# Head sums and low-rank products of an RWKV preparation as float32r parts, on one core of a Trainium2 chip

## The chip, the cores and the metric

The kernel runs on one core of a Trainium2 chip. The core has TensorE (PE, with its weight loads PEld), VectorE (DVE), ScalarE (ACT), GpSimdE (POOL) and the DMA queues, one of them issued by SyncE (SP). The metric is the device time of one execution in microseconds.

## The reference

One decoder layer: 512 tokens of width 1024, float32. A normed input is projected once; its columns feed a sparse attention mixer, an RWKV-7 mixer and two gates. The mixers are merged, projected, added to the input, and a gated MLP with a short convolution follows. What matters here is the preparation of the RWKV mixer (8 heads of 64):

```python
r, k, v, xw, xa, xg = jnp.split(xl, RWKV_SPLITS, axis=-1)
w = -jax.nn.softplus(-(w0 + jnp.tanh(xw) @ w2)) - 0.5
decay = jnp.exp(-jnp.exp(w.astype(jnp.float32)))
a = jax.nn.sigmoid(a0 + xa @ a2)
...
kk = k * k_k.reshape(H, N).astype(jnp.float32)
kk = kk / jnp.maximum(jnp.sqrt(jnp.sum(kk * kk, axis=-1, keepdims=True)), 1e-12)
k = k * (1.0 + (a - 1.0) * k_a.reshape(H, N).astype(jnp.float32))
...
y = y + jnp.sum(r * k * r_k, axis=-1, keepdims=True) * v
```

`tanh(xw) @ w2` and `xa @ a2` are the low-rank products (inner width 64 each). The two `jnp.sum` over the 64 channels of a head are the head sums: one for the norm of `kk`, one for the bonus.

## The kernel before

Activations lie feature-major: 128 features on the partitions, 512 tokens along the free side, so one tile holds two heads, and four pairs p = 0 to 3 hold the eight. Dense products (`dense_fm`) keep about float32 accuracy with float32r operands: weights and activations are split into a high part, rounded to float32r (`whi`, `hh`), and the rest (`wlo`, `hl`), and three products are added up, hi x hi, hi x lo and lo x hi. For one `dense_fm` that is 16 products that take `whi` and 8 that take `wlo`, 24 of 128x128 by 128x512. ScalarE makes `whi` and VectorE (at times GpSimdE) makes `wlo`, two buffers of each; SyncE's queue loads `raw` into three buffers.

The preparation runs over p. `front(p)` makes `k` (`kx`) by a dense product, then the two low-rank products into `ps_a` and `ps_b`: `wa` holds `w2` on partitions 0 to 63 and `a2` on 64 to 127, `xw` holds `tanh(xw)` and `xa` likewise, so each product uses 64 rows of the array. Then come the decay, its running sum along each chunk of 64 tokens (`cum`, by a scan), and its exponentials `ep` and `pi`. `norms(p)` squares `k` on ScalarE and multiplies the squares by `ones`, a 128x128 matrix with ones where two partitions belong to the same head: the head sum, spread over the head's partitions. `receptance(p)` and `values_of(p)` are dense products that give `rx` and `vx`. `values_tok(p)` transposes `vx`. `vectors(p)` makes `AR`, `bh` and the bonus sum (`tv` times `ones`, into `BO`). `gram(p)` transposes `bh` in sixteen 64-row operations, eight for each head of the pair, into one `ps_a` and one `ps_b` bank, and then multiplies `bh` by `AR` in sixteen 64-row products, first into another pair of `ps_a` and `ps_b`, then into two `ps_mm` banks; VectorE masks them into `AB`.

The program calls `front(0)`, `norms(0)`, `receptance(0)`, `values_of(0)`, and then for each p: `front(p+1)`, `norms(p+1)`, `values_tok(p)`, `vectors(p)`, `receptance(p+1)`, `gram(p)`, `values_of(p+1)`; one more dense product (`kcp`) comes at p = 2. In this part a scheduler orders each engine's instructions when the kernel is built; an engine runs its queue in that order. PSUM has two banks for `pa()` (`ps_a`), two for `pb()` (`ps_b`) and four for `mmb()` (`ps_mm`); a bank is free again when its last reader is done. After the preparation VectorE inverts the chunk matrices, while TensorE goes on with dense products, and from there on TensorE's order is mostly written out by hand.

In the profile nearly all matrix products have line L120 (the helper `mm`), ScalarE's activations L123 (`act`), VectorE's operations L126, L130, L132 and L135 (`tt`, `ts`, `stt`); L294 is the weight split on VectorE or GpSimdE, L540 the transposes of `vx`, L571 those of `bh`. `kc` holds the constants, `ones` among them.

Of the kernel before, what the change touches and what calls it, by code (L numbers as in the profile page):

```python
# [10 lines left out]
F32 = mybir.dt.float32  # L11
F32R = mybir.dt.float32r
I32 = mybir.dt.int32
AF = mybir.ActivationFunctionType
ALU = mybir.AluOpType
# [4 lines left out]
S = 512  # L20
# [27 lines left out]
NROWS = _n  # L48
NR0 = ROWS["ffn_norm_g"][0]
# [31 lines left out]
def hybrid_block(ctx: ExitStack, tc: tile.TileContext, A: dict, out: bass.AP):  # L81
    nc = tc.nc
# [16 lines left out]
    def pool(name, side="left"):  # L99
        cm = tc.tile_pool(name=name, bufs=1, side=side)  # L100
        return cm, cm.__enter__()

    def close(cm):
        cm.__exit__(None, None, None)


    def bank(tag, bufs, shape=(128, 512)):
        return ps.tile(list(shape), F32, name="ps_" + tag, tag=tag, bufs=bufs)

    def mmb():  # L110
        return bank("mm", 4)

    def pa():
        return bank("a", 2)

    def pb():
        return bank("b", 2)

    def mm(o, l, r, start, stop):
        te.matmul(o, lhsT=l, rhs=r, start=start, stop=stop)  # L120

    def act(o, i, f=AF.Copy, **kw):
        sc.activation(o, i, f, **kw)  # L123

    def tt(o, a, b, op):
        v.tensor_tensor(o, a, b, op=op)  # L126

    def ts(o, a, s1, s2, op0=ALU.mult, op1=ALU.add):
        if s2 is None:
            v.tensor_scalar(o, a, s1, None, op0=op0)  # L130
        else:
            v.tensor_scalar(o, a, s1, s2, op0=op0, op1=op1)  # L132

    def stt(o, a, s, b, op0=ALU.mult, op1=ALU.add):
        v.scalar_tensor_tensor(o, a, s, b, op0=op0, op1=op1)  # L135
# [3 lines left out]
    ident, mask, ones, cmask = kc[:, 0:128], kc[:, 128:256], kc[:, 256:384], kc[:, 384:416]  # L139
# [16 lines left out]
    for name in ("rwkv_mu", "rwkv_w0", "rwkv_a0", "rwkv_k_k", "rwkv_k_a", "rwkv_r_k", "rwkv_ln_g", "rwkv_ln_b"):  # L156
        r0, n = ROWS[name]
        src = A[name]
        if name == "rwkv_r_k":
            src = src.rearrange("l h d -> l (h d)")  # L160
# [7 lines left out]
    def col(name, i=0):  # L168
        r0, n = ROWS[name]
        return prm[:, r0 + i:r0 + i + 1]  # L170
# [35 lines left out]
    def norm_tiles(pool_):  # L206
        return (cp.tile([128, NT, 2], F32, name="ss", tag="ss"),
                [pool_.tile([128, D], F32, name="h", tag="h", bufs=NT) for _ in range(NT)])
# [120 lines left out]
    with tc.manual_schedule(engines={getattr(mybir.EngineType, e) for e in ("PE", "Activation", "DVE", "Pool")}):  # L329
# [18 lines left out]
        hi = wp.tile([128, KT, 128], F32R, name="whi", tag="whi", bufs=2)  # L348
        lo = wp.tile([128, KT, 128], F32R, name="wlo", tag="wlo", bufs=2)
# [43 lines left out]
    def run(g):  # L393
        while True:
            try:
                next(g)
            except StopIteration as e:
                return e.value

    def dense_fm_g(xh, xl, kt=KT):  # L400
        hi, lo = wnext(kt, 128)
        p = mmb()
        for k in range(kt):
            mm(p, hi[:, k], xh[:, k], k == 0, False)
            mm(p, hi[:, k], xl[:, k], False, False)
            if 4 * k == 3 * kt - 4:
                yield
        for k in range(kt):
            mm(p, lo[:, k], xh[:, k], False, k == kt - 1)
        return p  # L410

    def dense_fm(xh, xl, kt=KT):
        return run(dense_fm_g(xh, xl, kt))


    gp_cm, gp = pool("tb", "right")
# [3 lines left out]
    tp_cm, tp = pool("rtmp")  # L420
# [6 lines left out]
    BO = gp.tile([128, 4, S], F32, name="BO", tag="BO")  # L427
    PC = rp.tile([128, NH2, NCH], F32, name="PC")
    sg = gp.tile([128, S], F32, name="sg", tag="sg")
    g2 = gp.tile([128, 512], F32, name="g2", tag="g2")  # L430
    scanm = tp.tile([128, NCH, C], F32, name="scanm")
    v.memset(scanm, 1.0)
    v.memset(scanm[:, :, 0:1], 0.0)
    wa = tp.tile([128, 512], F32, name="wa")
    nc.gpsimd.dma_start(wa[0:64], A["rwkv_w2"][0])
    nc.gpsimd.dma_start(wa[64:128], A["rwkv_a2"][0])
    nc.gpsimd.dma_start(g2, A["rwkv_g2"][0])

    def shift_mix(p, m, dst):
        mu = col("rwkv_mu", m)  # L440
        act(dst, p, AF.Copy, scale=omm[:, m:m + 1])
        stt(dst[:, 1:], p[:, :-1], mu, dst[:, 1:])

    def t2(name, bufs=1):
        return tp.tile([128, S], F32, name=name, tag=name, bufs=bufs)

    xw = t2("xw")
    shift_mix(p0, 12, xw)
    act(xw[0:64], xw[0:64], AF.Tanh)
    shift_mix(dense_fm(hh, hl), 13, sg)  # L450

    act(sg, sg, AF.Tanh, scale=0.5)
    ts(sg, sg, 0.25, 0.25)


    prb = tp.tile([NROWS - NR0, 128], F32, name="prb")
    for name, (r0, n) in ROWS.items():
        if r0 >= NR0:
            r0 -= NR0
            src = A[name]  # L460
            if name.startswith("cmp_pe"):
                src = src.rearrange("l a d -> l (a d)")
# [2 lines left out]
                nc.gpsimd.dma_start(prb[r0:r0 + 1, 64:128], src)  # L465
            else:
                nc.gpsimd.dma_start(prb[r0:r0 + n], src[0].rearrange("(r p) -> r p", p=128))
    cr = tp.tile([88, 2, 128], F32, name="cr")
    nc.gpsimd.dma_start(cr[0:44, 0], A["conv_w"][0, 0].rearrange("(r p) -> r p", p=128))
    nc.gpsimd.dma_start(cr[44:88, 0], A["conv_w"][0, 1].rearrange("(r p) -> r p", p=128))  # L470
    nc.gpsimd.dma_start(cr[0:44, 1], A["conv_w"][0, 2].rearrange("(r p) -> r p", p=128))
# [1 line left out]
    def chunks(ap):  # L473
        return ap.rearrange("p (c t) -> p c t", t=C)
# [12 lines left out]
    L = {}  # L487


    def front(p):  # L490
        cs = slice(128 * p, 128 * p + 128)
        kx = t2("kx", 2)
        pk = dense_fm(hh, hl)
        zw, za = pa(), pb()
        mm(zw, wa[0:64, cs], xw[0:64], True, True)
        mm(za, wa[64:128, cs], xw[64:128], True, True)
        shift_mix(pk, 4 + p, kx)
        cl = t2("cl")
        act(cl, zw, AF.Tanh, scale=0.5, bias=w0h[:, p:p + 1])
        aa = t2("aa", 2)  # L500
        act(aa, za, AF.Tanh, scale=0.5, bias=a0h[:, p:p + 1])
        ts(cl, cl, -0.5 * DECAY, -0.5 * DECAY)
        cum = t2("cum")
        v.tensor_tensor_scan(out=cum, data0=scanm.rearrange("p c t -> p (c t)"), data1=cl, initial=0.0,
                             op0=ALU.mult, op1=ALU.add)
        ep = tp.tile([128, NCH, C + 1], F32, name="ep", tag="ep", bufs=2)
        v.memset(ep[:, :, 0:1], 1.0)
        act(ep[:, :, 1:], chunks(cum), AF.Exp)
        pi = t2("pi", 2)
        act(pi, cum, AF.Exp, scale=-1.0)  # L510
        v.tensor_copy(PC[:, p, :, None], ep[:, :, C:C + 1])
        L[p] = dict(kx=kx, aa=aa, ep=ep, pi=pi)

    def norms(p):
        kx = L[p]["kx"]
        kk = t2("kk", 2)
        act(kk, kx, AF.Square, scale=col("rwkv_k_k", p))
        ss = pa()
        mm(ss, ones, kk, True, True)
        rn = t2("rn", 2)  # L520
        ts(rn, ss, 1e-24, None, op0=ALU.max)
        act(rn, rn, AF.Ln)
        act(rn, rn, AF.Exp, scale=-0.5)
        L[p].update(kk=kk, rn=rn)

    def receptance(p):
        rx = t2("rx", 2)
        shift_mix(dense_fm(hh, hl), p, rx)
        L[p]["rx"] = rx

    def values_of(p):
        vx = t2("vx")
        shift_mix(dense_fm(hh, hl), 8 + p, vx)
        L[p]["vx"] = vx
# [9 lines left out]
                    pt[64 * cc:64 * cc + 64].rearrange("p (c r d) -> p c r d", r=2, d=DH)[:, :, r, :])  # L544

    def vectors(p):
        kx, aa, ep, pi, kk, rn, rx, vx = (L[p][k] for k in ("kx", "aa", "ep", "pi", "kk", "rn", "rx", "vx"))
        stt(AR[:, p, :, 1, :], chunks(rx), 1.0, ep[:, :, 1:], ALU.mult, ALU.mult)
        stt(kk, kx, col("rwkv_k_k", p), rn, ALU.mult, ALU.mult)
        stt(AR[:, p, :, 0, :], chunks(kk), -1.0, ep[:, :, 0:C], ALU.mult, ALU.mult)  # L550
        stt(kk, aa, 1.0, kk, ALU.add, ALU.mult)
        bh = tp.tile([128, NCH, 3, C], F32, name="bh", tag="bh")
        stt(bh[:, :, 0, :], chunks(kk), 0.5, chunks(pi), ALU.mult, ALU.mult)
        v.tensor_copy(bh[64:128, :, 2, :], bh[64:128, :, 0, :])
        ts(aa, aa, kah[:, p:p + 1], oma[:, p:p + 1])
        stt(kx, kx, 1.0, aa, ALU.mult, ALU.mult)
        stt(bh[:, :, 1, :], chunks(kx), 1.0, chunks(pi), ALU.mult, ALU.mult)
        tv = t2("tv")
        stt(tv, rx, col("rwkv_r_k", p), kx, ALU.mult, ALU.mult)
        L[p]["bh"] = bh  # L560
        bs = pa()
        mm(bs, ones, tv, True, True)
        tt(BO[:, p], bs, vx, ALU.mult)

    def gram(p):
# [19 lines left out]


    front(0)
    norms(0)
    receptance(0)
    values_of(0)  # L590
    late_params()
    for p in range(NH2):
        if p + 1 < NH2:
            front(p + 1)
            norms(p + 1)
        values_tok(p)
        vectors(p)
        if p + 1 < NH2:
            receptance(p + 1)
        gram(p)  # L600
        if p + 1 < NH2:
            values_of(p + 1)
        if p + 2 == NH2:
            kcp = dense_fm(hh, hl)
    dbg("AR", AR)
    dbg("BO", BO)
    close(tp_cm)

    m2_cm, m2 = pool("mix2")
    sg_cm, sgp = pool("sig")  # L610
    spare = sgp.tile([128, 2, 1024], F32R, name="spare", tag="sg0")
    sg1 = sgp.tile([128, 4, S], F32, name="sg1", tag="sg1")
    tp_cm, tp = pool("rinv")
# [163 lines left out]
    tp_cm, tp = pool("rseq")  # L777
# [455 lines left out]
    for m in range(KT):  # L1233
        cs = slice(128 * m, 128 * m + 128)
# [13 lines left out]
    ss, hs = norm_tiles(ntp)  # L1248
# [36 lines left out]
    with tc.manual_schedule(engines=KTS):  # L1285
        for t in range(NT):
            qs = slice(128 * t, 128 * t + 128)
            p = mmb()
# [13 lines left out]
        for pair in range(2):  # L1302
            cs = slice(256 * pair, 256 * pair + 256)
# [37 lines left out]
    for hf in range(2):  # L1341
        bo = dense_tok(512, aT[:, 0], aT[:, 1], NF)
        for t in range(NT):
            n = 256 if hf and t == NT - 1 else 512
            for c0 in range(0, 512, n):
                cs = slice(512 * hf + c0, 512 * hf + c0 + n)
# [30 lines left out]
```

## Time and profile before

| | |
|---|---|
| median of 3 runs | 848.09 us (847.67 to 848.52) |
| profiled execution | 847.76 us |
| its span | 846.0 us |
| granted TensorE clock | 1.00 |
| stretch with the changed code | about 18 to 125 us of the span |
| TensorE busy in 18 to 125 us | 106.31 us of 107.00 |
| VectorE, ScalarE busy there | 75.80 us, 66.89 us |

The span runs from the first to the last instruction. A row of the timeline has the start, the duration, the engine, the line, the operation, output <- inputs, the array's rows*columns for a product, the output's shape and type, and the count; in brackets stand the engine's idle time before it and what ended it. TensorE's records overlap: a product's duration includes its passage through the array, and the distance from one start to the next is what it costs in a dense sequence. Float32r operands of products are shown as f32. A float32 product has two records.

### The profile page before, as it was taken

To read this page: it belongs to the slowest core of one execution; us is meant where nothing else is said; L and a number is where in the kernel's file an instruction comes from. 1 tells how busy PE (TensorE), PEld (TensorE's weight loads), DVE (VectorE), ACT (ScalarE), POOL (GpSimd) and SP (SyncE) were. 2 spreads that over 40 slices of the span, in tenths; PEclk is the share of its full clock that TensorE was granted. 3 is DMA by queue.
4 is the path that set the end of the run, shared out by engine and by line. 5 is a ranking of instruction groups with operands and counts; after the bars stand their busy time and mean duration, and the time that the engine had idled before them with its cause. 6 is when DMAs were issued, how large, how long until landed. Compare 5 with 4: busy or idle time off the path is not lost.

```text
span 846.0 us, 12844 instructions
## 1 busy us (share of the span) xinstructions
PE 831.9 (98%) x5097; PEld 676.2 (80%) x5097; DVE 514.7 (61%) x998; ACT 405.7 (48%) x784; POOL 52.5 (6%) x69
## 2 busy tenths in 40 slices
PE   7999999999999999999999999999999999999998
PEld 6777778897777886777788888888888888888886
DVE  5477779963555678888675566666666666322222
ACT  6766645443545677767344454444444444221210
POOL 6200020140000110111000000000000000000000
PEclk9999999999999999999999999999999999999999
DMA  7432222335551320010167023333333332333421
GB/s 231 112 86 62 75 75 76 92 108 151 132 119 50 83 69 13 15 36 26 52 215 221 0 77 98 100 100 100 100 100 95 90 91 98 100 100 112 136 75 50
DMA packets 109104, 78.73 MB, mean 93 GB/s; under 512 B 3869, under 2 KB 97748, under 8 KB 109044
## 3 DMA queue, kind: packets, MB, share of 16 engines
q1 hardware_dynamic: 106512, 73.51, 29.8%
q0 software_dynamic: 1472, 1.86, 1.0%
q10 hardware_dynamic: 1060, 2.55, 1.0%
q8 instruction: 40, 0.66, 0.3%
q14 instruction: 20, 0.16, 0.1%
HBM read 74.56 MB, written 2.29 MB: 91 GB/s over the span
## 4 chain that ended last, share of the span: by engine, by line
PE 52%; DVE 0%; ACT 0%; DVEq 0%; issue 0%
PE ps_mm L120 52%; DVE hl L135 0%; PE ps_a L120 0%; PE ps_b L1181 0%; PE ps_a L200 0%; PE ps_mm L1181 0%; ACT hh L123 0%; PE ps_b L200 0%; DVE x L126 0%; DVEq L1373 0%; PE ps_a L1133 0%
## 5 line engine op out<-in xcount | busy, mean ns | idle before, releaser
L294 DVE TENSOR_TENSOR wlo<-raw,whi 128x1024 fp32r<-128x1024 f32 (+1 forms) x111 | 131.6, 1185 | 189.4 <-PE ps_mm L120 166.8
L120 PE MATMUL ps_mm<-hh,whi 128*128 128x512 f32 (+1 forms) x624 | 243.3, 392 | 0.4 <-ACT hh L123 0.3
L120 PE MATMUL ps_mm<-hl,whi 128*128 128x512 f32 (+1 forms) x624 | 240.9, 388 | 0.3 <-DVE hl L135 0.2
L123 ACT ACTIVATE whi<-raw 128x1024 fp32r<-128x1024 f32 (+3 forms) x124 | 123.4, 996 | 170.3 <-PE ps_mm L120 142.4
L120 PE MATMUL ps_mm<-hh,wlo 128*128 128x512 f32 (+1 forms) x624 | 151.8, 385 | 0.0
L120 PEld LDWEIGHTS ps_mm<-hh,whi 128*128 128x128 f32 x624 | 117.3, 188 | 27.3 <-issue 1.3
L120 PEld LDWEIGHTS ps_mm<-hl,whi 128*128 128x128 f32 x624 | 117.4, 188 | 24.1 <-DVE hl L135 1.0
L120 PEld LDWEIGHTS ps_mm<-hh,wlo 128*128 128x128 f32 x624 | 115.2, 188 | 23.3
L120 PE MATMUL ps_mm<-whi,aT 128*128 128x512 f32 x352 | 84.5, 390 | 0.0
L120 PEld LDWEIGHTS ps_mm<-whi,aT 128*128 128x128 f32 x352 | 65.9, 188 | 14.3 <-issue 0.4
L135 DVE SCALAR_TENSOR_TENSOR cgv<-ps_mm,cw,cgv 128x511 f32<-128x511 f32 (+1 forms) x88 | 65.4, 746 | 1.5
L123 ACT ACTIVATE cgv<-ps_mm,cw 128x512 f32<-128x512 f32 x44 | 34.3, 781 | 22.8 <-PE ps_mm L120 22.8
L120 PE MATMUL ps_mm<-wlo,aT 128*128 128x512 f32 x176 | 44.3, 390 | 0.0
L123 ACT ACTIVATE P<-P,nm 128x512 f32<-128x512 f32 (+3 forms) x64 | 35.4, 554 | 14.9 <-DVE nm L1155 14.9
L123 ACT ACTIVATE aT<-cgv 128x512 fp32r<-128x512 f32 x22 | 13.9, 631 | 56.8 <-DVE cgv L126 56.8
L120 PEld LDWEIGHTS ps_mm<-wlo,aT 128*128 128x128 f32 x176 | 33.1, 188 | 6.9
L123 ACT ACTIVATE cgv<-cgv 128x512 f32<-128x512 f32 x22 | 13.9, 632 | 43.9 <-DVE cgv L135 43.8
L294 POOL TENSOR_TENSOR wlo<-raw,whi 128x512 fp32r<-128x512 f32 (+3 forms) x13 | 20.4, 1573 | 203.6 <-PE ps_mm L120 147.9
L1155 DVE CUSTOM_DVE_ANT_0 P<-ps_a,AB 128x512 f32<-128x512 f32 (+3 forms) x64 | 29.4, 484 | 4.2 <-PE ps_a L120 3.7
L126 DVE TENSOR_TENSOR x<-x,ps_mm 128x512 f32<-128x512 f32 (+1 forms) x17 | 11.1, 656 | 23.9 <-PE ps_mm L120 22.7
L126 DVE TENSOR_TENSOR aT<-cgv,aT 128x512 fp32r<-128x512 f32 x22 | 15.2, 693 | 14.7 <-ACT aT L123 14.7
L120 PE MATMUL ps_a<-KH,qst 128*128 128x512 f32 (+3 forms) x64 | 21.3, 349 | 1.5 <-DVE nm L1155 0.9
(356 smaller groups left out, 1205.5 us busy)
## 6 DMA issues: line engine op xcount, KB each, us to landing
raw<-in_w_up_dram SPq DMA_DIRECT2D x44, 512.0 KB, 3.8
raw<-in_w_in_dram SPq DMA_DIRECT2D x38, 512.0 KB, 3.9
raw<-in_w_down_dram SPq DMA_DIRECT2D x22, 512.0 KB, 3.6
raw<-in_w_out_dram SPq DMA_DIRECT2D x8, 512.0 KB, 3.7
xt<-in_x_dram SPq DMA_DIRECT2D x4, 512.0 KB, 5.7
raw<-in_cmp_w_k_dram SPq DMA_DIRECT2D x4, 512.0 KB, 4.0
raw<-in_cmp_w_v_dram SPq DMA_DIRECT2D x4, 512.0 KB, 4.4
raw<-in_w_proj_b_dram SPq DMA_DIRECT2D x8, 256.0 KB, 2.7
```

The lines of the kernel that those rows point to most:

```text
L120: te.matmul(o, lhsT=l, rhs=r, start=start, stop=stop)
L123: sc.activation(o, i, f, **kw)
L126: v.tensor_tensor(o, a, b, op=op)
L135: v.scalar_tensor_tensor(o, a, s, b, op0=op0, op1=op1)
L294: eng.tensor_tensor(lo, raw, hi.bitcast(F32), op=ALU.subtract)
L1155: v.tensor_tensor_reduce(out=P[:, i], in0=sp[:, N * (i - i0):N * (i - i0) + N], in1=BT[:, h, 384 - 128 * qt:512], scale=-1.0, scalar=-NEG, ...
```

## The change

Products with `ones` and with `wa` become float32r products of parts. `parts(hi, lo, src)` copies `src` to float32r on ScalarE and subtracts that copy on VectorE. `head_sums(x)` splits `x` into a tile `xp2` (one buffer, for both kinds of sum) and adds up two products with `onr`, a float32r copy of `ones`, which is exact. The low-rank products take three float32r products each, from `wap` and `xwp`, with the two halves alternating. `receptance(0)` is called ahead of `norms(0)`. To make room in SBUF, `xw`, `kk` and `tv` share one buffer, `cum` is written over `cl`, the squares go into `rn`, `wa` uses the buffer of `vx`, `prb` and `cr` that of `bh`, and the high part of `wa` that of `g2`, which is loaded after the preparation, no longer at its start.

```diff
-    g2 = gp.tile([128, 512], F32, name="g2", tag="g2")
...
-    wa = tp.tile([128, 512], F32, name="wa")
+    xwp = tp.tile([128, 2, S], F32R, name="xwp")
+    wap = [gp.tile([128, S], F32R, name="wa_hi", tag="g2"), tp.tile([128, S], F32R, name="wa_lo")]
+    onr = tp.tile([128, 128], F32R, name="onr")
+    act(onr, ones)
+
+    def parts(hi, lo, src):
+        act(hi, src)
+        tt(lo, src, hi.bitcast(F32), ALU.subtract)
+
+    wa = tp.tile([128, 512], F32, name="wa", tag="vx")
     nc.gpsimd.dma_start(wa[0:64], A["rwkv_w2"][0])
     nc.gpsimd.dma_start(wa[64:128], A["rwkv_a2"][0])
-    nc.gpsimd.dma_start(g2, A["rwkv_g2"][0])
...
-    xw = t2("xw")
+    xw = t2("kk")
     shift_mix(p0, 12, xw)
     act(xw[0:64], xw[0:64], AF.Tanh)
+    parts(xwp[:, 0], xwp[:, 1], xw)
+    parts(*wap, wa)
...
-    prb = tp.tile([NROWS - NR0, 128], F32, name="prb")
+    rows = tp.tile([128, 3, 128], F32, name="rows", tag="bh")
+    prb, cr = rows[0:NROWS - NR0, 2], rows[0:88, 0:2]
...
-        mm(zw, wa[0:64, cs], xw[0:64], True, True)
-        mm(za, wa[64:128, cs], xw[64:128], True, True)
+        for i, (a, b) in enumerate(((0, 0), (0, 1), (1, 0))):
+            mm(zw, wap[a][0:64, cs], xwp[0:64, b], i == 0, i == 2)
+            mm(za, wap[a][64:128, cs], xwp[64:128, b], i == 0, i == 2)
...
-        cum = t2("cum")
+        cum = cl
...
+    def head_sums(x):
+        xp2 = tp.tile([128, 2, S], F32R, name="xp2", tag="xp2")
+        parts(xp2[:, 0], xp2[:, 1], x)
+        ss = pa()
+        mm(ss, onr, xp2[:, 0], True, False)
+        mm(ss, onr, xp2[:, 1], False, True)
+        return ss
+
     def norms(p):
         kx = L[p]["kx"]
-        kk = t2("kk", 2)
-        act(kk, kx, AF.Square, scale=col("rwkv_k_k", p))
-        ss = pa()
-        mm(ss, ones, kk, True, True)
         rn = t2("rn", 2)
+        act(rn, kx, AF.Square, scale=col("rwkv_k_k", p))
+        ss = head_sums(rn)
         ts(rn, ss, 1e-24, None, op0=ALU.max)
...
-        tv = t2("tv")
+        tv = t2("kk")
         stt(tv, rx, col("rwkv_r_k", p), kx, ALU.mult, ALU.mult)
         L[p]["bh"] = bh
-        bs = pa()
-        mm(bs, ones, tv, True, True)
+        bs = head_sums(tv)
         tt(BO[:, p], bs, vx, ALU.mult)
...
     front(0)
+    receptance(0)
     norms(0)
-    receptance(0)
     values_of(0)
...
     close(tp_cm)
 
+    g2 = gp.tile([128, 512], F32, name="g2", tag="g2")
+    nc.gpsimd.dma_start(g2, A["rwkv_g2"][0])
```

More of the change, by code (lines that the diff above doesn't have):

```diff
@@ L467, in hybrid_block @@
                 nc.gpsimd.dma_start(prb[r0:r0 + n], src[0].rearrange("(r p) -> r p", p=128))
-    cr = tp.tile([88, 2, 128], F32, name="cr")
     nc.gpsimd.dma_start(cr[0:44, 0], A["conv_w"][0, 0].rearrange("(r p) -> r p", p=128))
@@ L523, in norms @@
         act(rn, rn, AF.Exp, scale=-0.5)
-        L[p].update(kk=kk, rn=rn)
+        L[p]["rn"] = rn
     def receptance(p):
@@ L546, in vectors @@
     def vectors(p):
-        kx, aa, ep, pi, kk, rn, rx, vx = (L[p][k] for k in ("kx", "aa", "ep", "pi", "kk", "rn", "rx", "vx"))
+        kx, aa, ep, pi, rn, rx, vx = (L[p][k] for k in ("kx", "aa", "ep", "pi", "rn", "rx", "vx"))
+        kk = t2("kk")
         stt(AR[:, p, :, 1, :], chunks(rx), 1.0, ep[:, :, 1:], ALU.mult, ALU.mult)
```

## The prediction

> **What bounds the kernel.** I read the page, then the stretch from 18 to 125 us, in which the changed code lies: its engines' busy time and who waited for whom. After it the built order of both kernels is the same on every engine.
>
> ```profile
> PE 831.9 (98%) x5097; PEld 676.2 (80%) x5097; DVE 514.7 (61%) x998; ACT 405.7 (48%) x784; POOL 52.5 (6%) x69
> 18.00:125.00 107.00, 106.31 (x598) 80.76 (x597) 75.80 (x123) 66.89 (x96) 11.91 (x18) 1.00 0.32 85
> PE ps_b L540 <- DVE vx L135: 0.2, 1, 0.2
> PE ps_mm L120 <- DVE AB L126: 0.2, 1, 0.2
> DVE wlo L294 <- PE ps_mm L120: 10.8, 4, 2.8
> ```
>
> The second row gives busy time in the order PE, PEld, DVE, ACT, POOL. TensorE is busy for 106.31 of 107.00 us at the full clock and waits twice for 0.2 us; VectorE has 31 us free and waits 10.8 us in four places for TensorE. So what counts is how long TensorE's own queue takes. The change removes a little there, and moves products to other places in the queue, and that has to be priced too. The profiled execution took 847.76 us (span 846.0, 1.76 around it); the median of the runs is 848.09, 0.33 more. A difference under 0.2% (1.7 us) I count as no change: about what a measurement can tell.
>
> **Head sums.** Eight float32 products with `ones` become sixteen float32r products with `onr`.
>
> ```profile
> 53.74 0.39 PE L120 MATMUL ps_mm<-hh,whi 128*128 128x512 f32 x1
> 53.97 0.39 PE L120 MATMUL ps_mm<-hl,whi 128*128 128x512 f32 x1
> 54.43 1.02 PE L120 MATMUL ps_a<-kk,kc 128*128 128x512 f32 x2
> 55.29 1.02 PE L120 MATMUL ps_a<-tv,kc 128*128 128x512 f32 x2
> ```
>
> The spacing of starts is the price, since ends overlap: a float32r product takes 0.23 us, a float32 one 0.86 (54.43 to 55.29, two records). Each sum falls from 0.86 to 0.46: 8 x 0.40 = **-3.2 us**.
>
> **Low-rank products.** Two float32 products on 64 rows, in the two halves of the array, become six float32r ones.
>
> ```profile
> 29.41 1.98 PE L120 MATMUL ps_mm<-hh,wlo 128*128 128x512 f32 x8
> 31.31 0.69 PE L120 MATMUL ps_a<-xw,wa 64*128 64x512 f32 x1
> 31.32 0.69 PE L120 MATMUL ps_b<-xw,wa 64*128 64x512 f32 x1
> 31.84 0.59 PE L120 MATMUL ps_a<-xw,wa 64*128 64x512 f32 x1
> 32.37 0.50 PE L120 MATMUL ps_mm<-hh,whi 128*128 128x512 f32 x1
> 32.70 0.39 PE L120 MATMUL ps_mm<-hl,whi 128*128 128x512 f32 x1
> ```
>
> Both halves start together, so a pair costs as one. The eight products from 29.41 would end their slots at 31.23; the next dense product stands at 32.37, with 0.10 lost before 32.70. That is 1.24 us for a pair worth 0.86: going into half-array products and out again costs 0.38. I call this a crossing; its lower bound is the plain gaps, 0.1 in and 0.1 out. Afterwards three pairs of 0.23 and a crossing: 1.07, so 4 x 0.17 = **-0.7 us**. Float32r products on 64 rows are not in this trace. With the smaller crossing it is -1.4; with the six one after another, 1.76 each time, it is +2.1. I take side by side, as the float32 rows show.
>
> **The first head sum** stands in the middle of the next dense product and waits for its operand.
>
> ```profile
> 33.86 0.40 PE L120 MATMUL ps_mm<-hh,whi 128*128 128x512 f32 x1
> 34.40 1.13 PE L120 MATMUL ps_a<-kk,kc 128*128 128x512 f32 x2
> ```
>
> It was due at 34.09 and starts at 34.40. `receptance(0)` now comes first, and the sum stands behind its whole dense product (24 slots): **-0.3 us**.
>
> **What moves: the Gram products.** Here each 64-row operation of one head has a partner of the other head in the other half of the array.
>
> ```profile
> 59.79 0.22 PE L571 MATMUL ps_b<-kc,bh 64*128 64x64 f32 x1
> 59.79 0.22 PE L571 MATMUL ps_a<-kc,bh 64*128 64x64 f32 x1
> 59.85 0.22 PE L571 MATMUL ps_b<-kc,bh 64*128 64x64 f32 x1
> 60.39 0.27 PE L120 MATMUL ps_b<-AR,bh 64*128 64x128 f32 x1
> 60.40 0.27 PE L120 MATMUL ps_a<-AR,bh 64*128 64x128 f32 x1
> 60.50 0.27 PE L120 MATMUL ps_b<-AR,bh 64*128 64x128 f32 x1
> ```
>
> A pair of transposes takes 0.06 us, a pair of products two records of 0.11, so 0.22. In the changed build the bonus sum needs the `ps_a` bank for longer, and the scheduler splits the pairs. TensorE's order there for p=1, and the same for p=2 (ps_b and ps_mm_870 are the first half, ps_a and ps_mm_871 the second):
>
> ```
> ps_b<-kc,bh x8 | ps_b<-AR,bh x2 | ps_a<-xp2,onr | ps_a<-kc,bh x8 | ps_b<-AR,bh x2
> ps_mm_870<-AR,bh | ps_a<-xp2,onr | ps_mm_871, 870, 871, 870, 871 | ps_a<-AR,bh x4 | ps_mm_870, 871
> ```
>
> Sixteen transposes in 16 slots, not 8: +0.5 us (0 if a single one is cheaper than a pair). The 16 products take 13 slots, not 8: 2 + 2 + 1, then after the second sum 3 (two of them pairs), 4 (the last beside ps_mm_870) and 1; 5 x 0.22 = +1.1. Two full-array sums inside the half-array work: two more crossings, +0.76 (0.4 by the bound). That is 2.36 each for p=1 and p=2 (from 1.5). For p=0 one sum lies between and one slot is added: 0.38 + 0.22 = 0.6 (from 0.4). For p=3 the sum stands ahead of whole pairs: nothing. Together **+5.3 us** (3.4 to 5.3).
>
> **New operands, new waits.** Each sum waits for a copy on ScalarE and a subtraction on VectorE:
>
> ```profile
> 23.14 0.63 ACT L123 ACTIVATE xw<-xw 64x512 f32<-64x512 f32 x1
> 115.93 0.75 DVE L135 SCALAR_TENSOR_TENSOR tv<-rx,prm,kx 128x512 f32<-128x512 f32 x1
> 117.73 0.74 DVE L135 SCALAR_TENSOR_TENSOR vx<-ps_mm,prm,vx 128x511 f32<-128x511 f32 x1
> 120.08 0.69 DVE L126 TENSOR_TENSOR BO<-ps_a,vx 128x512 f32<-128x512 f32 x1 [1.61 <-PE ps_a L120]
> 118.53 0.66 PE L540 MATMUL ps_b<-kc,vx 128*128 128x128 f32 x4 [0.25 <-DVE vx L135]
> 119.02 1.02 PE L120 MATMUL ps_a<-tv,kc 128*128 128x512 f32 x2
> 107.32 0.75 DVE L135 SCALAR_TENSOR_TENSOR rx<-ps_mm,prm,rx 128x511 f32<-128x511 f32 x1 [1.31 <-ACT rx L123]
> ```
>
> Ten subtractions at about 0.69 and ten copies at about 0.63 make VectorE 82.7 and ScalarE 73.2 of 107: neither becomes the bound. What can hurt is the place. At p=3 `vx` is already 0.25 us late. Now `bh` and `tv` follow it, then copy and subtraction: about 2 x 0.75 + 0.63 + 0.69 = 2.8 us from its end to the low part, of which TensorE covers 0.49 (the transposes, 118.53 to 119.02) and 0.23 (the high part). That is 2.1 us of stall if `vx` stays as late. But `rx` no longer stands behind the second Exp and its table load (the 1.31 above), and `vx` moves ahead of those 1.5 us; against that stand two subtractions, 1.4. So `vx` comes about 1.4 earlier, and TensorE itself later by what its Gram products lose; I put 0.5 there. At p=0 the two sums of the loop stand behind all of `vectors(0)` on VectorE; I put 0.5 there too, one low part that is not covered (0.69 less 0.23). Waits **+1.0 us** (0 if both are covered; 3.1 with 2.1 at p=3 and both sums of p=0 bare). Behind a waiting sum on TensorE stand the Gram operations, and behind a waiting subtraction on VectorE the `BO` and `AB` products that free their banks.
>
> **Edits at nothing.**
>
> ```profile
> 24.21 1.06 ACT L123 ACTIVATE whi<-raw 128x1024 fp32r<-128x1024 f32 x1 [0.44 <-PE ps_mm L120]
> 20.47 0.52 POOL L436 DMA_DIRECT2D wa<-in_rwkv_a_dram  x1
> DMA to landing us min/median/max: 4.9/5.0/5.1
> L120 PE MATMUL ps_b<-sg,g x32: 274/275/276, 223.9 to 307.6; 128*128 128x128 f32 x32
> ```
>
> `wa` lands at about 25.6 us (20.47 + 5.1). ScalarE now waits for it after the Tanh, with the copy of `xw`, the `sg` step and the next weight split behind: that split goes from 24.21 to about 27.6, and its product starts at 32.37. If the 3.7 us of cover were gone, each us would count. `g2` loads after the fourth low-rank products instead of at the start, over 100 us ahead of its first reader at 223.9; GpSimd has nothing due when it waits. The shared tiles (`xw`, `kk` and `tv`; `cl` and `cum`; `rows` and `bh`; `wa` and `vx`) have their users one after another on VectorE or far apart.
>
> **Sum:** -3.2 - 0.7 - 0.3 + 5.3 + 1.0 = +2.1 us. On the profiled 847.76 that is 849.9; on the median of the runs **850.2 us**, slower by 0.25%. By the bounds: from -1.5 (-3.2 - 1.4 - 0.3 + 3.4) to +7.0 (-3.2 + 2.1 - 0.3 + 5.3 + 3.1). A shift here goes to the end one to one, as TensorE's order behind it is the same and its work as dense.
>
> **Rivals.**
> 1. *The halves overlap all the same.* TensorE might run the split halves beside each other, though they stand apart. Then only five crossings remain: -3.2 - 1.4 - 0.3 + 1.0 = -3.9, 844.2 us. It decides if the 13 slots of a Gram step take no longer than the 8. For it: half-array pairs do run side by side. Against: the starts of the rows above keep the order of the queue. 0.15.
> 2. *Weights are laid bare.* The second low-rank pair starts 0.53 after the first (31.31 to 31.84) where half of 0.86 would do: 0.10 lost. If every operation that follows one in its own half pays that, about 32 of them in each of two Gram steps add 6.4: 856.6 us. Against: dense products run every 0.23 us on the same rows. 0.10. The Trainium skill has it as a rule ("TensorE: Matmul & The Clock Gate", Part 3: Packing small matmuls): a weight load overlaps running products only when its row group differs. The dense rows here speak against it.
> 3. *The chain at p=3 decides.* `vx` stays as late as it is and the split of `tv` stalls TensorE for the whole 2.1 us, not 0.5: 851.8. It decides if `vx` ends after the products ahead of its transposes. 0.15.
> 4. *The float32r halves do not pair*, so the low-rank part does not do what it says: +2.1 in place of -0.7, 853.0 us. 0.10.
>
> **Numbers.** The forecast has 0.50, with a range of its own of 848.7 to 851.7; of it 0.22 lies within 0.2% of 848.09 (up to 849.8) and 0.28 above. Rivals 2 to 4 add 0.35 to slower, rival 1 gives 0.14 to faster and 0.01 to same. Faster 0.14, same 0.23, slower 0.63. The range 845.5 to 854.0 leaves out rival 2 and most of rival 1.
>
> **What would show it.** Sums 0.46 us apart from their neighbours in the dense product; low-rank groups of about 1.07; the steps from the first transpose to the last Gram product longer by over 2 us at p=1 and p=2 and unchanged at p=3; waits of TensorE for VectorE or ScalarE on `ps_a` of 0.3 to 0.6. The forecast is wrong if the Gram steps stay at 2.5 us plus two sums (rival 1), or if the distance between half-array operations of one half is over 0.11 per record (rival 2).

## The result, and the profile after

The changed kernel takes 850.64 us (median of 7 runs, 850.57 to 850.92), the kernel before 847.67 beside it (7 runs): ratio 1.0034, 95% interval 1.0022 to 1.0045. It is slower by 3.0 us; the forecast was 2.1 on the median, 850.2. The profiled execution's span grew from 846.0 to 848.8 us.

The page's first part and the stretch from 18 to 125 us (busy time of PE, PEld, DVE, ACT, POOL, then clock and DMA) of the changed kernel, and TensorE's waits from 19 to 135 us (us in total, times, longest):

```profile
PE 832.6 (98%) x5105; PEld 679.1 (80%) x5105; DVE 521.3 (61%) x1008; ACT 412.4 (49%) x795; POOL 52.6 (6%) x69
18.00:125.00 107.00, 105.27 (x578) 82.83 (x578) 79.62 (x128) 70.45 (x103) 10.62 (x16) 1.00 0.30 83
PE ps_a L120 <- DVE xp L126: 1.0, 1, 1.0
PE ps_b L120 <- ACT UV L123: 0.5, 1, 0.5
PE ps_a L120 <- ACT xp L123: 0.2, 1, 0.2
PE ps_mm L120 <- DVE AB L126: 0.2, 1, 0.2
```

TensorE has one more microsecond of gaps: where it once waited twice for 0.2 us it now waits 1.9 in four places, and two of the four are sums (`xp` is the operand tile `xp2`). It has 20 records fewer in the stretch because the work behind has moved out of it; in the whole kernel it has 8 more, as each of the four low-rank groups has six records where it had four.

The first low-rank product of each p is a mark in TensorE's order, and VectorE's first transposition of the inversion ends the stretch. Before (the mark of p=0, 31.31, stands in the prediction), then after:

```profile
50.79 0.69 PE L120 MATMUL ps_a<-xw,wa 64*128 64x512 f32 x1
73.26 0.69 PE L120 MATMUL ps_a<-xw,wa 64*128 64x512 f32 x1
95.74 0.69 PE L120 MATMUL ps_a<-xw,wa 64*128 64x512 f32 x1
124.41 2.05 DVE L623 STREAM_TRANSPOSE inv<-AB 32x1024 f32<-32x1024 f32 x1
```

```profile
31.44 0.49 PE L120 MATMUL ps_a<-xwp,wa_hi 64*128 64x512 f32 x1
49.91 0.49 PE L120 MATMUL ps_a<-xwp,wa_hi 64*128 64x512 f32 x1
50.24 0.39 PE L120 MATMUL ps_a<-xwp,wa_hi 64*128 64x512 f32 x1
50.25 0.39 PE L120 MATMUL ps_b<-xwp,wa_hi 64*128 64x512 f32 x1
50.79 0.66 PE L557 MATMUL ps_b<-kc,vx 128*128 128x128 f32 x4
73.86 0.49 PE L120 MATMUL ps_a<-xwp,wa_hi 64*128 64x512 f32 x1
98.22 0.49 PE L120 MATMUL ps_a<-xwp,wa_hi 64*128 64x512 f32 x1
127.84 2.04 DVE L642 STREAM_TRANSPOSE inv<-AB 32x1024 f32<-32x1024 f32 x1
```

The distances from mark to mark, and what the prediction's terms make of each (a low-rank group -0.17, a sum -0.40, the Gram and wait terms where they belong; the stretch to the second mark also has the first stall):

| stretch | holds | before | after | change | by the terms |
|---|---|---|---|---|---|
| 1st to 2nd mark | norm 0 | 19.48 | 18.47 | -1.01 | -0.88 |
| 2nd to 3rd | norm 1, bonus 0, Gram 0 | 22.47 | 23.95 | +1.48 | +0.13 |
| 3rd to 4th | norm 2, bonus 1, Gram 1 | 22.48 | 24.36 | +1.88 | +1.39 |
| 4th to the inversion | norm 3, bonus 2 and 3, Gram 2 and 3 | 28.67 | 29.62 | +0.95 | +1.49 |
| sum | | | | +3.30 | +2.13 |

The half-array parts do pair (50.24 and 50.25), and the group takes 0.88 us to the transposes of `vx` where it took 1.06 (50.79 to the 51.85 of before's `vx` transposes).

The Gram step of p=1, from the first transpose to the next dense product: before it is 2.48 us long (the first two rows), after 5.33 (81.78 to 87.11):

```profile
82.15 0.27 PE L571 MATMUL ps_b<-kc,bh 64*128 64x64 f32 x1
84.63 0.50 PE L120 MATMUL ps_mm<-hh,whi 128*128 128x512 f32 x1
```

```profile
80.97 0.42 PE L120 MATMUL ps_a<-xp,onr 128*128 128x512 f32 x1
81.22 0.63 PE L120 MATMUL ps_mm<-hh,wlo 128*128 128x512 f32 x2
81.78 0.71 PE L588 MATMUL ps_b<-kc,bh 64*128 64x64 f32 x8
82.33 0.66 PE L120 MATMUL ps_b<-AR,bh 64*128 64x128 f32 x4
82.92 0.49 PE L120 MATMUL ps_a<-xp,onr 128*128 128x512 f32 x1
83.35 0.52 PE L588 MATMUL ps_a<-kc,bh 64*128 64x64 f32 x5
83.65 0.37 PE L120 MATMUL ps_b<-AR,bh 64*128 64x128 f32 x1
83.71 0.35 PE L588 MATMUL ps_a<-kc,bh 64*128 64x64 f32 x3
...
84.20 0.38 PE L120 MATMUL ps_mm<-AR,bh 64*128 64x128 f32 x2
84.52 0.50 PE L120 MATMUL ps_a<-xp,onr 128*128 128x512 f32 x1
84.95 0.93 PE L120 MATMUL ps_mm<-AR,bh 64*128 64x128 f32 x10
...
87.11 0.50 PE L120 MATMUL ps_mm<-hh,whi 128*128 128x512 f32 x1
```

Inside a dense product a sum's part costs 0.25 us (80.97 to 81.22). Inside the Gram step it costs 0.43 from its own start (82.92 to 83.35, 84.52 to 84.95), with 0.10 to 0.15 of gap ahead of it. Without the 0.46 of the two parts the step lasts 4.87 us, 2.39 more than before. Eight transposes of one half take 0.55 us, 0.069 each.

### The profile page after: what moved, and what is told of

Same layout as the page of the kernel before. It is cut to its first block, busy times and chain, and to the rows that moved or that the text cites. A ratio compares the mean times of both kernels' runs of the same rounds, so it can differ in the third digit from the quotient of the medians.

```text
span 848.8 us, 12887 instructions
## 1 busy us (share of the span) xinstructions
PE 832.6 (98%) x5105; PEld 679.1 (80%) x5105; DVE 521.3 (61%) x1008; ACT 412.4 (49%) x795; POOL 52.6 (6%) x69
## 4 chain that ended last, share of the span: by engine, by line
PE 52%; DVE 0%; ACT 0%; DVEq 0%; issue 0%
PE ps_mm L120 51%; DVE hl L135 0%; PE ps_a L120 0%; PE ps_b L1200 0%; PE ps_a L200 0%; PE ps_mm L1200 0%; ACT hh L123 0%; PE ps_b L200 0%; DVE x L126 0%; DVEq L1392 0%; PE ps_a L1152 0%
```

## The experiments

Theory A is the prediction's: what the change loses, it loses in Gram steps whose pairs are split and crossed by the bonus sum. Theory B: the bonus sum's operands come late, and the split only fills time in which TensorE would wait.

**Whole pairs, the sum moved behind.** `head_sums(tv)` is divided: the parts are still made in `vectors(p)`, the two products and `BO` move to a function `bonus(p)`.

```diff
         gram(p)
         if p + 1 < NH2:
             values_of(p + 1)
+            bonus(p)
```

(At p=3 `bonus(p)` is called ahead of `gram(p)`.)

> The changed kernel with all its float32r parts; only the place of the bonus sum's two products differs: at p=0, 1 and 2 they stand behind the next values product, and the Gram pairs are whole again; p=3 is as in the changed kernel. Theory A (the split pairs and the crossings inside the Gram steps are the loss): the Gram steps go back to about 2.5 us, 2.4 less at p=1 and p=2 and 0.9 less at p=0, so 5.7 less in all, about 845 us, faster than before by 2 to 3. Theory B (the late operands of the sums are the loss, and the split only fills time in which TensorE would have waited): the Gram steps get shorter but waits of like size come up at the sums, 849 to 851 us.

850.93 us, ratio 1.0043 (1.0031 to 1.0056). That lies in theory B's range, but the marks say more: 31.39, 49.86, 72.57 and 95.40. The Gram step of p=1 is 2.48 us again, and up to the fourth mark the kernel is 2.8 us ahead of the changed one (A: 0.9 + 2.4, less 0.85 for a longer wait at a norm sum, 2.5). All of it, and the gain of the Gram step of p=2, is lost at p=3. VectorE and GpSimd there, TensorE's waiting row, and the clock in a window of this kernel (the number ahead of the last two; busy times of PE, PEld, DVE, ACT, POOL stand before it):

```profile
117.47 2.34 POOL L294 TENSOR_TENSOR wlo<-raw,whi 128x1024 fp32r<-128x1024 f32 x1 [20.48 <-PE ps_mm L120]
117.51 2.85 DVE L135 SCALAR_TENSOR_TENSOR kk<-rx,prm,kx 128x512 f32<-128x512 f32 x1
121.08 1.52 PE L120 MATMUL ps_a<-xp,onr 128*128 128x512 f32 x2 [2.77 <-ACT xp L123]
122.00:126.00 4.00, 4.00 (x41) 3.56 (x43) 1.20 (x2) 1.67 (x4) 0.00 (x0) 0.50 0.23 70
```

In this version a weight split on GpSimd starts 0.04 us before VectorE's step for the bonus, and that step takes 2.85 us for 0.75: it ends 0.55 after GpSimd's. TensorE waits 2.77 us, and from near the end of that wait its clock is halved for 6.8 us (about 120.7 to 127.5, by windows of 1 us). That the two engines hold each other up is so far a guess from their times; a run below tests it.

**Whole pairs, the sum in its old place.**

```diff
-        gram(p)
+        with tc.manual_schedule(engines={mybir.EngineType.PE}):
+            bonus(p)
+            gram(p)
```

> The changed kernel with all its float32r parts and the bonus sum in its old place ahead of the Gram step, but TensorE's order there is fixed by hand so that the sum's two products come first and the Gram pairs are whole. Theory A: as with the sum moved behind, about 845 to 846 us, since the pairs are whole. Theory B: the two products now wait bare for copy and subtraction, 1 to 2 us in front of each Gram step, and the time stays at 850 to 851 us: then the split was no loss against whole pairs in this place.

852.17 us, ratio 1.0055 (1.0043 to 1.0068): theory B, in this place. TensorE at p=1:

```profile
82.75 0.49 PE L120 MATMUL ps_a<-xp,onr 128*128 128x512 f32 x1 [0.95 <-ACT xp L123]
84.09 0.50 PE L120 MATMUL ps_a<-xp,onr 128*128 128x512 f32 x1 [0.85 <-DVE xp L126]
```

It waits 1.80 us for the two parts here, and the stretch from the third mark to the fourth is 24.63 us, with the split 24.36. The scheduler's split was no mishap: it put Gram work where TensorE would otherwise have stood still.

**The split alone,** in the float32 kernel before: the inner loops of `gram` turned round, one head after the other.

```diff
-        for c in range(NCH):
-            for r in range(2):
+        for r in range(2):
+            for c in range(NCH):
...
-            for i in range(4):
-                for r in range(2):
+            for r in range(2):
+                for i in range(4):
```

> The kernel before, all float32, with only the two inner loops of the Gram steps turned round, so that the eight transposes, and each four products, of one head come ahead of those of the other and few pairs are left. No operands change and no sum stands in between. By the prediction's price (8 more slots of 0.06 and up to 8 more of 0.22 in each of four steps, less a slot or two where the ends meet): 7 to 9 us slower, 855 to 857. Rival: a half that stands alone takes half of a pair's time, or halves overlap across the order: 847.7 to 849.5.

850.73 us, ratio 1.0038 (1.0025 to 1.0050): 3.2 more, under half of the expected least. Parts of the step of p=0:

```profile
59.75 0.52 PE L571 MATMUL ps_b<-kc,bh 64*128 64x64 f32 x5
60.06 0.27 PE L571 MATMUL ps_a<-kc,bh 64*128 64x64 f32 x1
60.12 0.22 PE L571 MATMUL ps_b<-kc,bh 64*128 64x64 f32 x1
60.17 0.22 PE L571 MATMUL ps_a<-kc,bh 64*128 64x64 f32 x1
...
63.12 0.50 PE L120 MATMUL ps_mm<-hh,whi 128*128 128x512 f32 x1
```

The queue has eight `ps_b` transposes and then eight `ps_a`, yet the first `ps_a` starts when three of the `ps_b` are still to come, and from there the halves run side by side. The step is 3.37 us, 0.89 more than whole pairs, where the slot count gives 2.24. This is rival 1's mechanism: an operation of one half passes three of the other that stand ahead of it in the queue. The section on the kernel before says that an engine runs its queue in order; between TensorE's two halves that does not hold. In the changed kernel a full-array sum stands between the halves, and nothing of the other half starts ahead of it (82.92, then 83.35). Behind the sum the halves overlap a little there too: a `ps_b` product starts at 83.65, ahead of three `ps_a` transposes (83.71) that the queue has before it. So the slot count came out right for the step as a whole (2.39 for 2.36), not slot by slot.

**Shared tiles and order, float32 arithmetic.** First the changed kernel with all products in float32 again (`xwf` and `waf` are plain float32 copies), then the kernel before with the calls of p=0 in the new order:

```diff
-        for i, (a, b) in enumerate(((0, 0), (0, 1), (1, 0))):
...
+        mm(zw, waf[0:64, cs], xwf[0:64], True, True)
+        mm(za, waf[64:128, cs], xwf[64:128], True, True)
...
-        ss = head_sums(rn)
+        ss = pa()
+        mm(ss, ones, rn, True, True)
...
-        bs = head_sums(tv)
+        bs = pa()
+        mm(bs, ones, tv, True, True)
```

```diff
     front(0)
-    norms(0)
     receptance(0)
+    norms(0)
```

> The changed kernel's shared tiles, its late load of g2 and its order of receptance(0), but with every head sum and low-rank product as one float32 product as before. All theories here: sharing and order cost nothing, 0.3 us less from the first sum, 847 to 848 us. If the shared tiles add waits, 848.5 or more, and part of the loss is theirs.

> The kernel before with one edit: receptance(0) ahead of norms(0). No tile is shared, all arithmetic is float32. The float32 kernel with shared tiles and this order was 1.7 us slower than before; TensorE waited 0.8 us for the square of the norm at p=1 and 0.9 for vx at p=3. Theory C (the order is the cause: vectors(0) runs one dense product later on VectorE, and the next steps stand behind it): 849 to 849.6 us, with the same waits. Theory D (the shared tiles are the cause): 847 to 847.7 us.

849.26 us (1.0011 to 1.0029 times before) and 849.37 (1.0012 to 1.0029). So the sharing costs nothing that shows, and the order costs 1.7 us: theory C. TensorE in the kernel with the order alone:

```profile
55.15 1.12 PE L120 MATMUL ps_a<-kk,kc 128*128 128x512 f32 x2 [0.82 <-ACT kk L123]
120.42 0.66 PE L540 MATMUL ps_b<-kc,vx 128*128 128x128 f32 x4 [0.93 <-DVE vx L135]
```

From the first mark to the second it gains 0.42 us, from the second to the third it loses 1.08: `norms(0)` ends one dense product later, so does all of `vectors(0)` on VectorE, and the square of `norms(1)` waits for a `kx` that stands behind it.

**The collision taken away.** The version with the sum moved behind, and the weight split on VectorE:

```diff
-        yield from rows(w_in, O_Q, 512, eng=[v, pool_, ("spare", pool_), v])
+        yield from rows(w_in, O_Q, 512, eng=[v, v, ("spare", pool_), v])
```

> The kernel with the bonus sum moved behind the values product (p=0 to 2), and one weight split, the subtraction of 2.34 us that stood on GpSimd at 117.5 in that kernel, put on VectorE instead. In that kernel the VectorE step for the bonus at p=3 (kk from rx and kx) took 2.85 us in place of 0.75 while GpSimd worked, TensorE waited 2.77 us for it, and its granted clock was then 0.50 for about 6 us. Theory A with this collision: the step is 0.75 again, TensorE's wait falls under 1 us, the clock stays at 1.00, and the time is about 845 to 846 us. If the wait and the low clock have another cause, 850 to 851 us, as with the split on GpSimd.

848.21 us, ratio 1.0008 (0.9999 to 1.0017). The bonus step is 0.74 us, TensorE's longest wait at p=3 is 0.66, the clock 1.00, and 2.7 us are back: the collision is shown. It was not all: waits of 0.96 and 1.05 us at the norm sums of the loop's first two passes and 1.2 in all at p=3 are left, and the time stays 2 to 3 us above A's. Most of these are waits for copies and subtractions, so theory B has a share in what is left.

With the sum of p=3 behind its Gram products too, and the weight split on GpSimd:

```diff
-        if p + 1 == NH2:
-            bonus(p)
         gram(p)
         if p + 1 < NH2:
             values_of(p + 1)
-            bonus(p)
+        bonus(p)
```

> As with the bonus sum moved behind the values product, but at p=3 too it stands behind everything else, after the Gram products. The GpSimd split stays. Theory A with the collision: the slow VectorE step at p=3 now has the Gram step as cover, so TensorE waits about 1 us at most, the clock stays at 1.00, and the time is 845 to 847 us. If the saving of the whole pairs is not real: 850 or more.

851.20 us, ratio 1.0043 (1.0031 to 1.0056). That is not because whole pairs save nothing: the Gram step was no cover. VectorE's step took 2.84 us again, ScalarE's copy of `kk` came late, and behind that copy stand the evacuations `UV` that free the `ps_b` bank of the Gram products: TensorE waited 3.41 us for them, and near the end of that wait its clock was halved, for 3.4 us. The expectation had left out who stands behind the waiting copy.

**The bonus sum in float32,** the rest as changed:

```diff
-        bs = head_sums(tv)
+        bs = pa()
+        mm(bs, ones, tv, True, True)
```

> The changed kernel with only the bonus sum as one float32 product again (no copy, no subtraction for it); the norm sums and low-rank products stay float32r. The Gram pairs are whole, and the sum stands in the dense product as before. Theory A: against the changed kernel it saves the 5.7 us of the Gram steps and loses the 1.6 us of four sums, about 846 to 846.5 us. If the whole pairs bring nothing: 851 to 852 us.

845.38 us, ratio 0.9973 (0.9963 to 0.9984): faster than the changed kernel and than the one before, and 0.6 under what theory A gave. It is 5.3 less than the changed kernel though four sums take 0.40 more. One wait of 0.6 is left in the stretch, and the step of p=1 is whole:

```profile
81.26 0.27 PE L589 MATMUL ps_b<-kc,bh 64*128 64x64 f32 x1
81.26 0.27 PE L589 MATMUL ps_a<-kc,bh 64*128 64x64 f32 x1
...
83.74 0.50 PE L120 MATMUL ps_mm<-hh,whi 128*128 128x512 f32 x1
```

So two parts for the bonus sum, alone, cost 6.9 us (5.3 + 1.6) to save 1.6.

**The crossing by itself.** TensorE's order fixed by hand inside `gram(p)` only, so that pairs are whole and the sum falls between them:

```diff
-        gram(p)
+        with tc.manual_schedule(engines={mybir.EngineType.PE}):
+            gram(p)
```

> The changed kernel with TensorE's order fixed by hand only inside each Gram step, so that the pairs stay whole and the two float32r products of the bonus sum fall where the scheduler puts them: at p=1 and p=2 both inside the step, each breaking one pair; at p=0 one of them. This takes the split away and keeps the crossings. By the prediction's price of 0.38 a crossing, the step at p=1 without its waits is 2.48 + 0.46 for the sum + 2 x 0.38 + about 0.3 for two broken pairs = 4.0 us, against 5.33 in the changed kernel and 2.94 with nothing inside. If the split costs only the 0.9 us that it cost alone, and the crossings the rest, the step is 4.4 to 4.7. Waits of the sums may come on top; 849 to 851.5 us in all.

852.65 us, ratio 1.0058 (1.0044 to 1.0072). At p=1 TensorE waited in the step for 0.76 and 0.78 us (for `xp`, and for `BO`, which frees the sum's `ps_a` bank), and then the clock halved in mid-step, so the length there says nothing. At p=2 the clock stayed at 1.00:

```profile
107.41 0.27 PE L588 MATMUL ps_b<-kc,bh 64*128 64x64 f32 x1
108.05 0.51 PE L120 MATMUL ps_a<-xp,onr 128*128 128x512 f32 x1 [0.37 <-ACT xp L123]
...
109.53 0.50 PE L120 MATMUL ps_a<-xp,onr 128*128 128x512 f32 x1
110.82 0.37 PE L120 MATMUL ps_a<-AR,bh 64*128 64x128 f32 x1 [0.78 <-DVE BO L126]
...
112.80 0.50 PE L120 MATMUL ps_mm<-hh,whi 128*128 128x512 f32 x1
```

The step is 5.39 us long, 4.24 without the two waits shown, and the second product waited a little as well: VectorE's subtraction for it ended at 109.48. That is under the 4.4 to 4.7 of a cheap split and near the 4.0 of the prediction's price. So in the changed kernel's order the split costs 1.1 us or more a step (5.3 less 4.24), and not only the 0.89 that it costs alone.

What a crossing costs, at p=1 and the full clock:

```profile
82.68 0.49 PE L120 MATMUL ps_a<-xp,onr 128*128 128x512 f32 x1 [0.76 <-ACT xp L123]
83.11 0.27 PE L588 MATMUL ps_a<-kc,bh 64*128 64x64 f32 x1
```

Out of the sum takes 0.43 for a product of 0.23, so 0.20. The way in cannot be read in this kernel, as its products waited for their parts. With the 0.10 to 0.15 of the changed kernel a crossing is 0.30 to 0.35: the 0.38 of the prediction is of the right size, a little high.

**Low rank alone,** in the changed kernel:

```diff
-        ss = head_sums(rn)
+        ss = pa()
+        mm(ss, ones, rn, True, True)
...
-        bs = head_sums(tv)
+        bs = pa()
+        mm(bs, ones, tv, True, True)
...
     front(0)
-    receptance(0)
     norms(0)
+    receptance(0)
```

> The low-rank products alone: the changed kernel with both head sums as one float32 product and norms(0) ahead of receptance(0) as in the kernel before; shared tiles and the splitting of xw and wa stay. By the prediction four groups of 1.07 in place of 1.24 us: 0.7 us less than before, 847.0 us; each distance from one low-rank group to the next is that of before less 0.17. If the smaller price of a crossing holds, 846.3. If sharing tiles costs something by itself, over 847.7.

849.69 us, ratio 1.0024 (1.0016 to 1.0033), and not for the low-rank products: the marks are 50.50, 72.79 and 95.08, distances of 22.29 and 22.29 where 22.47 and 22.48 were, so 0.18 and 0.19 less. Then the collision came again (the bonus step 2.40 us, TensorE's wait 1.75).

**The best version.** Float32 where nothing covers the parts, two parts behind the values product where something does; then the same without GpSimd's split, by the edit shown above:

```diff
+        if p in {0, 3}:
+            L[p]["xp2"] = None
+            bonus(p)
+        else:
+            xp2 = tp.tile([128, 2, S], F32R, name="xp2", tag="xp2")
+            parts(xp2[:, 0], xp2[:, 1], tv)
...
+        if xp2 is None:
+            mm(bs, ones, L[p]["tv"], True, True)
...
         if p + 1 < NH2:
             values_of(p + 1)
+        if p not in {0, 3}:
+            bonus(p)
```

> Best version so far by the experiments: the changed kernel with the bonus sum as one float32 product at p=0 and p=3, where nothing covers copy and subtraction, and as two float32r products behind the values product at p=1 and p=2, where a whole product covers them. The Gram pairs are whole everywhere. Against the version with all four bonus sums in float32 (845.4 us) two sums save 0.40 each: 844.6 us. If at p=2 the extra VectorE work delays the bonus step of p=3 into the GpSimd split again (TensorE idle over 2 us, clock 0.50), 848 to 850 us.

> The version with the bonus sum in float32 at p=0 and p=3 and in two parts behind the values product at p=1 and p=2, with one further edit: the weight split that stood on GpSimd at 115.66 there (2.34 us) is put on VectorE. In that version the bonus step of p=3 on VectorE took 2.84 in place of 0.75 and TensorE waited 2.19 us for it. Theory A with the collision: the step is 0.75 again, TensorE's wait for it is gone, the clock stays at 1.00, and the time is 844 to 845.3 us, the fastest of all versions. If the collision was not the cause, or the extra 1.22 us of VectorE takes its place: 847 to 849.

848.83 us with the collision (1.0000 to 1.0017) and 845.26 without (ratio 0.9971, 0.9959 to 0.9982). The eleven times with it lie between 847.02 and 850.23, with a mean clock of 0.999 in the shortest and 0.996 in the longest. The shortest is the profiled one, whose clock is 1.00 throughout the stretch, so about 1.8 us of the 3.6 come without any fall of the clock; that the rest is the clock is likely, but not shown. The step for the bonus of p=3 on VectorE, first with GpSimd's split beside it, then without:

```profile
115.66 2.34 POOL L294 TENSOR_TENSOR wlo<-raw,whi 128x1024 fp32r<-128x1024 f32 x1 [20.21 <-PE ps_mm L120]
115.70 2.84 DVE L135 SCALAR_TENSOR_TENSOR kk<-rx,prm,kx 128x512 f32<-128x512 f32 x1
```

```profile
115.99 0.74 DVE L135 SCALAR_TENSOR_TENSOR kk<-rx,prm,kx 128x512 f32<-128x512 f32 x1
```

That is 2.5 us faster than before, and no more than the version with all four bonus sums in float32 (their intervals overlap).

## Why the prediction was right, step by step

The direction and the size came from the right place: savings of about 4, a loss in the Gram steps of over 5. Its steps against the trace:

- Head sums, 0.46 for 0.86: right as a price of TensorE's slots (a part costs 0.23 to 0.25 in a dense product). Low rank, -0.17 a group: right, -0.18 and -0.19 when alone. Rival 4 falls: the halves pair.
- Gram steps at p=1 and p=2, 2.36 forecast, 2.39 measured at p=1 and 2.37 at p=2 (5.32 us, before 2.49). At p=0, from 59.10 to 62.75 with one part inside, 3.65 - 0.23 - 2.48 = 0.94, forecast 0.6. Together that is 5.7 for 5.3. Rival 1 falls: its mechanism exists, but with sums between the halves the step does not stay at 2.5 us and two parts. Rival 2 falls: a transpose that follows one in its own half costs 0.069 us, 0.01 more than a pair. The Trainium skill ("TensorE: Matmul & The Clock Gate", Part 3: Packing small matmuls) has the rule that a weight load overlaps running products only when its row group differs; these rows speak against it.
- Waits, +1.0: undersized, and at the wrong place. Put down were 0.5 at p=0 and 0.5 at p=3. This row of the changed kernel is the norm sum's low part at p=0 of the loop:

```profile
56.76 0.51 PE L120 MATMUL ps_a<-xp,onr 128*128 128x512 f32 x1 [0.96 <-DVE xp L126]
```

  It was due at about 55.63 (two products behind 55.17), and two later gaps of 0.1 to 0.2 follow: about 1.4 us. At p=3 the wait for `vx` is gone and `UV` holds TensorE up for 0.53 instead; rival 3 falls.
- The first stall, -0.3 for `receptance(0)` ahead of `norms(0)`: as the price of the new order the term had the wrong sign. The gain itself is there (0.42 in the float32 kernel up to the second mark). The step that failed is that it counted the sum that moves and not the chain behind it (`rn`, then all of `vectors(0)`). In all the order costs 1.7 us in the float32 kernel. In the changed kernel it was not undone alone, so how much of the 1.4 us at p=0 is its doing stays open.

By the table the misses are +1.35 and +0.49 in the middle stretches, -0.13 and -0.54 in the outer ones, +1.2 together; about 0.6 of the loss was regained behind the inversion (span +2.8), and where was not followed up. So the total came out nearer than its terms, and that is luck. The prediction put the split down to the `ps_a` bank, which the bonus sum holds for longer. The runs with whole pairs show that the sum's parts come late as well: with the sum ahead of the pairs TensorE waits 0.22 us for them at p=0, 1.80 at p=1 and 1.55 at p=2, and with the sum between the pairs it waits for a part (0.76 at p=1) and for the bank (0.78). So the split (850.64), the bare wait (852.17) and the sum between whole pairs (852.65, with 3.4 us at half the clock) are three ways to pay for a late sum. Which of the two, part or bank, the scheduler went by is not shown.

## What to carry to other kernels

Splitting an operand to save 0.4 us of TensorE puts a copy and a subtraction, 1.3 us, ahead of the product: do it where a whole product stands between, and leave the others in float32. Even there it gained nothing clear here over four bonus sums in float32 (845.26 and 845.38 us). When a step is called later, follow what hangs on its result on every engine, not only the slot it leaves. A version that is microseconds ahead meets other engines' work at new places: look in its trace for an instruction that takes several times its usual duration before the idea is given up.

## What the runs showed of the hardware

- A VectorE step that reads two tensors from SBUF (`kk` from `rx` and `kx`) took 2.84 and 2.85 us for 0.75 when GpSimd's subtraction had started 0.04 us earlier, and 2.40 when 0.49 earlier. When VectorE's step had started first, by 0.53 us (the bonus sum in float32), it took 0.74 and GpSimd's subtraction 2.42. Steps that read PSUM and SBUF were not slowed (`BO`, 0.69, inside GpSimd's 2.35 from 122.47 in the changed kernel). The Trainium skill ("SBUF — State Buffer", Who interferes with whom) says this: a VectorE instruction with two SBUF inputs and a GpSimd one that reads SBUF exclude each other, and the first keeps the other out for its whole length. These rows agree.
- TensorE's granted clock fell to 0.50 near the end of waits of 2.77 and 3.41 us, and also 0.2 us after the second of two waits of 0.76 and 0.78 within 4 us. It stayed at 1.00 after one wait of 2.19, and after two of 0.95 and 0.85 within 4 us. So the length of the waits alone does not tell whether it falls. It stayed low for 6.8, 3.4 and 3.4 us. The Trainium skill ("TensorE: Matmul & The Clock Gate", Part 1: The HAM clock gate) puts the fall behind an idle window of about 3.4 us; the waits of 2.77 and of 0.76 and 0.78 were shorter, and the measurement decides.
- A half-array operation started ahead of three earlier ones of the other half in the queue (60.06 in the split alone); a full-array product between the halves was not passed.
